# Four mixed layers on one core: value and receptance weights of the second recurrent layer split ahead of time, in earlier feed-forward stages

## The chip, the cores and the metric

The kernel runs on one core of a Trainium2 chip. The core has five engines with a queue of instructions each: PE (the matrix engine, with its weight loads shown as PEld), DVE (elementwise work on 128 partitions), ACT (activations and copies), POOL, and SP, which here only issues DMAs. The metric is the device time of one execution in microseconds, as the median of three runs. The profile is one further execution, taken by the hardware profiler; its own time stands in the table below.

## The reference

The model is a trunk of four residual layers over a sequence of 256 positions with 1024 channels, all in float32. Layers 0 and 3 mix tokens with a recurrence (RWKV-7), layer 1 with stick-breaking attention, layer 2 with sparse attention; a SwiGLU feed-forward block with 2816 hidden channels follows each layer. What matters here is the recurrent mixer. It shifts the input by one position, mixes it with the unshifted one six ways, and multiplies three of the mixtures by 1024x1024 weights:

```
xm = h[:, :, None, :] + (shifted - h)[:, :, None, :] * mix
rkv = jnp.einsum('bsjd,jde->bsje', xm[:, :, :3], w_rkv)
r, k, v = rkv[:, :, 0], rkv[:, :, 1], rkv[:, :, 2]
...
v = v + (v_first - v) * jax.nn.sigmoid(v0 + (xv @ v1) @ v2)   # second recurrent layer
...
state = state * w_t - sa * (kk_t * a_t) + v_t * k_t           # step by step, per head
```

The kernel computes the step-by-step state in chunks of 64 positions: within a chunk a small triangular system is inverted, then the chunks follow each other.

## The kernel before, in words

**Stages.** The program goes through eight stages: mixer 0, feed-forward 0, mixer 1, and so on to feed-forward 3. Activations lie with channels on the partitions. All matrix weights come from DRAM as pieces of 128 x 1024 float32 (512 KB), in the order in which they are needed.

**Two ways to multiply.** A product with float32 weights can be done directly: `product` loads a piece as it is (tile `raw`) and PE multiplies float32 by float32. Or it is done with split operands: a value is taken apart into a high part, rounded to the format fp32r, and the rest, its low part; three fp32r matmuls (high by high, high by low, low by high) replace one float32 matmul (`mm3`, called by `gemm2`). For this `piece` loads a piece into `raw`, ACT or DVE copies it into `wh` (the high part, a CAST), and DVE subtracts the high part from the piece into `wl`. `raw`, `wh` and `wl` have three buffers each. In both recurrent layers the receptance product (tiles `rp`, weights of key `rr`) and the key product (`kp`) use split operands, and the value product (`vp`, key `rv`) is the direct one.

**The inverse.** After the products that make them, the chunk matrices `sc` are masked, and a chain of 62 small DVE operations (tiles `inv` and `xtmp`) inverts their 32x32 blocks. Two DVE transposes end it (`xd`, then `XT`), and PE takes the blocks further with small matmuls (`cmb`). Then the chain over the chunks runs (`xu`, `qu`, `pS`, `Y`), and the output product (`po`) ends the stage. While DVE works on the inverse, PE has the value product and the value's layout changes (`qct`, `vtok`, `bv`).

**Order.** Every operation is recorded first, with what it depends on. The order in which the recorded operations are emitted, the engine of each operation that two engines can do (CAST by ACT or DVE, for instance), and the buffer of each tile stand in one packed table, ORDER, read by `schedule`. Where the table holds an empty turn, `emit` puts in two short matmuls whose result nobody uses (`warm_o`), to keep PE busy. Each engine works its own list strictly in order, and waits for others by semaphores. All DMAs are on SP's queue: a DMA there that waits for a buffer holds back all DMAs behind it.

**Names.** In the order's rows and the profile, out<-in stands for the tile that is written and those that are read; the program's lines for these operations are all in one helper, L571.

Of the kernel before, what the change touches and what calls it, by code (L numbers as in the profile page):

```python
# [24 lines left out]
P = 128  # L25
# [277 lines left out]
c-rk+OKe={b@uuH|Ni&=m^*Xl{U$j>4u?YyDU#wtq9l^yLlPyKl3%iE*|IGsshhfX(k4NgxLKrW<HRXY6m?q!LHs~cv_KXO(mF*K0lIOJHYkv0*Pz|D-  # L303
6flD`u+Fbp(MvhS6!7yCg(o>*E#1q-
#KUKhe~ff^nlPqCvqbH*OECg!HJy6iJZuZoXCls$cdcDiJZuZoX7{|<V%?oIgt}NkrO$Q|A#U?<d#Kb7{)_U#G3bt0x2Kzvq2`n1*FrF6Jcms!Zc0CamJi>8&_s%nno^
H)PgbH&OMfcMA0<^zw}GSrTzT_-7w4Ltm$Q3&+rbzVQ<dWZQSXht_RV0R5MJ&-
7*Z<ivm3=I$l=Sop5S;dQvxZbG+9xqac&Z1sQ*=Qtds{Yc{HtsoD$^Bs5W|6)RUQGn?I97h+Xg5n?R}1G8nD&x^_(!+pkC40@0`O%7yU2s@LpsnHl469wTKi}ku8^g^K
^3?qu9%x1@V_``0d6*m8-*W1^orl$H^?aihB^t2U-$;oQht5qP`Y}KoHUOr#^dNIH$va{JNZ^#Vi-R^j2a@_Mg!5xvy)gvB;U-
+FbTA%$a=ls*Uo^|!W_Vu!5aVZVSU*s@7#IdoAA;i(qW7g4=u{>(>9sTg|5EFNI|6p(b^}WmdA})8Iy>#pO-QDN!93AcM@_TaQ2ETdb;qN{C@WGYKN9Q2xJ8W%jZF6mH
<$H{=>+AzEG0oVS`yUjGY~riq<-&rxdFX+$)6>(EwOg&uWTDXM)R_=0Yd0G8TD?=NjgODpRZUdO^|~plT+{4Qu~gDDEfaChwzs##kg-  # L310
5FeABsh&2>G`xOB<=oNMpyIgWktBA~RjZEWiL`SU=+*^PeRU~{_8mY3N=MfeM2{`?RkgzNTPfs+U!tnu-
VDca*>?KWFl>i1j90D2X+RG<39M6H&?Ri<8Ng+frybDV^0j+U{QX)-mqpm5AERy}v{fC2u7@B8I4gZuLO%#5qBJh{OIlWWpo_65zzY-FnQY*?AA=%UnL=+F0urMWp>LI
)@7I84`pS^eTg9a?WU8fM2V7RSc)GLwLkWNc+coX(ZY12zL;{XQ$yfuj7?t1M!dbNN_UIVzRlzF~IG4%gNkhEpspElmZy%#0#qGP3%8v6`(i1;sEN8ZFi=7<r>wt$N-
#XUtw%S@{jdmJyr4`_MO+o8~jms4a(Pzwc(VS#zpX3d5`6!NL4%`8;Qq6^58x*5T`yU)ETTv05N2lFfTV&(j72jrDC?h_94Zzx-
# [260 lines left out]
def trunk(ctx: ExitStack, tc: tile.TileContext, xT_in, wts, lora_in, consts_in, id32_in, outT, order, layers=None):  # L575
# [358 lines left out]
    def rwkv(j, layer, after):  # L934
# [910 lines left out]
```

## Time and profile before

| what | value |
|---|---|
| median of three runs | 1280.58 us (1278.81 to 1280.99) |
| the profiled execution's own time | 1280.3 us |
| its span, first to last instruction | 1278.5 us |
| PE busy | 1268.4 us |
| DVE busy | 1146.4 us |
| ACT busy | 699.7 us |
| DMA: bytes moved | 221.89 MB, 174 GB/s on average |

The span is read as a row of stages, each with its own busiest engine. The stages' limits, found from the first and last instructions of each, are about: mixer 0 from 8 to 175 us, feed-forward 0 to 350, mixer 1 to 455, feed-forward 1 to 630, mixer 2 to 758, feed-forward 2 to 932, mixer 3 to 1100, and feed-forward 3 to the end. Busy time of matmuls is modelled at its end: a row's mean duration holds the overlap with its neighbours, so a price for PE's time is read from stretches of equal matmuls in the chain of waits, where start follows start.

### The profile page before, as it was taken

How to read it: one execution, taken by the hardware profiler on the slowest of the kernel's cores; microseconds unless marked ns; L12 is line 12 of the kernel's file. 1: busy time of each engine (PE TensorE's matmuls, PEld its weight loads, DVE VectorE, ACT ScalarE, POOL GpSimd, SP SyncE). 2: the span in 40 equal slices, each digit the busy share in tenths (PEclk: the TensorE clock that was granted, in tenths of full speed). 3: DMA queues.
4: the chain of work that ended last, by engine and by line, in shares of the span. 5: the costliest groups of instructions: out<-in, count | busy, mean ns of one | idle time of the engine just before them, and what ended most of it. 6: DMA issues, size and time to landing. Idle time of an engine off the chain costs nothing.

```text
span 1278.5 us, 25690 instructions
## 1 busy us (share of the span) xinstructions
PE 1268.4 (99%) x10362; PEld 1153.1 (90%) x10362; DVE 1146.4 (90%) x1912; ACT 699.7 (55%) x1254; POOL 14.1 (1%) x18
## 2 busy tenths in 40 slices
PE   8999999999999999999999999999999999999998
PEld 7897899999988999999999899999988888999998
DVE  8998999898889989997899998988799998999885
ACT  5976655443355653443467965454249757654521
POOL 0020000000000000000000000000000000000000
PEclk9999999999999999999999999999999999999999
DMA  6432166665564465565646555655743331666654
GB/s 242 145 125 92 53 212 193 216 191 184 193 199 150 143 204 186 197 211 181 211 151 195 169 170 197 212 196 169 232 160 132 131 96 54 213 203 196 198 185 158
DMA packets 62567, 221.89 MB, mean 174 GB/s; under 512 B 7280, under 2 KB 8688, under 8 KB 62192
## 3 DMA queue, kind: packets, MB, share of 16 engines
q1 hardware_dynamic: 62448, 220.25, 52.6%
q8 instruction: 81, 1.33, 0.4%
q14 instruction: 38, 0.31, 0.1%
HBM read 217.08 MB, written 1.05 MB: 171 GB/s over the span
## 4 chain that ended last, share of the span: by engine, by line
PE 94%; DVE 3%; DMA 2%; issue 1%; ACT 0%; SPq 0%; DVEq 0%; ACTq 0%
PE up L571 18%; PE gate L571 18%; PE dn L571 17%; PE po L571 7%; PE vp L571 4%; PE kp L571 3%; PE rp L571 3%; PE vps L571 3%; PE qk L571 3%; PE z L571 2%; DMA raw<-in_wts_dram 1%; PE sc L571 1%; PE Y L571 1%; PE lora_in L571 1%; DVE wl L571 1%; PE attn_o L571 1%
## 5 line engine op out<-in xcount | busy, mean ns | idle before, releaser
L571 DVE TENSOR_TENSOR wl<-raw,wh 128x1024 fp32r<-128x1024 f32 x285 | 346.9, 1221 | 38.7 <-ACT wh L571 32.4
L571 ACT CAST wh<-raw 128x1024 fp32r<-128x1024 f32 x190 | 199.2, 1050 | 183.7 <-PE dn L571 92.7
L571 PE MATMUL dn<-h,wh 128*128 128x512 f32 (+1 forms) x726 | 233.3, 376 | 0.0
L571 PE MATMUL dn<-h,wl 128*128 128x256 f32 x704 | 191.2, 273 | 0.8 <-DVE wl L571 0.8
L571 PEld LDWEIGHTS dn<-h,wh 128*128 128x128 f32 x726 | 135.7, 189 | 18.0 <-DVE h L571 0.2
L571 PE MATMUL up<-xg,wring 128*128 128x512 f32 x704 | 141.8, 328 | 0.0
L571 PE MATMUL gate<-xg,wring 128*128 128x512 f32 x704 | 140.2, 328 | 0.0
L571 PEld LDWEIGHTS dn<-h,wl 128*128 128x128 f32 x704 | 135.5, 192 | 1.2 <-DVE wl L571 1.1
L571 PE MATMUL up<-xg,wh 128*128 128x512 f32 x352 | 123.6, 382 | 0.0
L571 PE MATMUL gate<-xg,wh 128*128 128x512 f32 x352 | 123.1, 382 | 0.0
L571 PEld LDWEIGHTS up<-xg,wring 128*128 128x128 f32 x704 | 106.1, 191 | 9.3
L571 PEld LDWEIGHTS gate<-xg,wring 128*128 128x128 f32 x704 | 106.1, 191 | 9.1
L571 DVE TENSOR_TENSOR wring<-raw,wring 128x1024 fp32r<-128x1024 f32 x88 | 107.0, 1220 | 7.0 <-ACT wring L571 6.0
L571 PE MATMUL up<-xg,wl 128*128 128x256 f32 x352 | 96.0, 273 | 0.0
L571 PE MATMUL gate<-xg,wl 128*128 128x256 f32 x352 | 96.0, 273 | 0.0
L571 PE MATMUL qk<-xg,wh 128*128 128x256 f32 (+1 forms) x384 | 86.1, 313 | 0.0
L571 DVE CAST wh<-raw 128x1024 fp32r<-128x1024 f32 x95 | 65.3, 688 | 18.0 <-PE dn L571 12.0
L571 ACT COPY gus<-gate 128x256 f32<-128x256 f32 x88 | 32.3, 373 | 88.6 <-PE gate L571 73.8
L571 PEld LDWEIGHTS gate<-xg,wh 128*128 128x128 f32 x352 | 66.6, 189 | 9.2
L571 PEld LDWEIGHTS up<-xg,wh 128*128 128x128 f32 x352 | 66.6, 189 | 9.2
L571 ACT CAST wring<-raw 128x1024 fp32r<-128x1024 f32 x58 | 60.8, 1052 | 20.7 <-DMA raw<-in_wts_dram 15.5
L571 PE MATMUL qk<-xg,wl 128*128 128x256 f32 x256 | 70.3, 275 | 0.0
(321 smaller groups left out, 2674.7 us busy)
## 6 DMA issues: line engine op xcount, KB each, us to landing
raw<-in_wts_dram SPq DMA_DIRECT2D x397, 512.0 KB, 4.1
lora<-in_lora_dram SPq DMA_DIRECT2D x2, 1536.0 KB, 9.9
rhl<-qa SPq DMA_DIRECT2D x32, 64.0 KB, 3.4
lora<-in_lora_dram SPq DMA_DIRECT2D x2, 512.0 KB, 5.4
lg<-in_lora_dram SPq DMA_DIRECT2D x8, 128.0 KB, 3.7
inv<-in_id_dram SPq DMA_DIRECT2D x2, 512.0 KB, 4.2
out_dram<-xt SPq DMA_DIRECT2D x3, 256.0 KB, 2.4
xt<-in_xT_dram SPq DMA_DIRECT2D x1, 660.0 KB, 4.8
```

The costliest lines, as they stand in the source:

```text
L571: getattr(getattr(nc, o.eng), method)(*map(real, args), **{k: real(a) for k, a in kw.items()})
```

## The change

**Parking.** A new function `park` does the split of a weight piece early: it loads the piece, casts and subtracts as `piece` does, but into one tile of 128 x 2 x 1024 (1 MB, in the groups of buffers named s0 and s1), and a DMA writes this tile to a place in DRAM. A table AHEAD says which pieces are parked in which feed-forward stage: four value pieces in feed-forward 0, four value and two receptance pieces in feed-forward 1, six receptance pieces in feed-forward 2. That is all eight `rv` and all eight `rr` pieces of layer 3. When `piece` is asked for a parked key, it issues two DMAs of 512 KB, one into `wh` and one into `wl`; no CAST and no subtraction follows.

**Value product.** In layer 3 (j == 1) the value product becomes a `gemm2` with split operands. Its input `xv` is split into high and low parts in a new tile `xvhl`, four times 128 x 512. The first recurrent layer keeps the direct product.

**Tiles.** The inputs of the gate product, `xg`, get a tile of their own in group s0, in both recurrent layers; `XT` moves from s0 to s1, and the two `yhl` tiles swap s0 and s1. The table ORDER is new as a whole.

```diff
     def piece(key, raw=None, parts=None):
 
+        if key in parked:
+            h, l = T([PIECE], "wh", "wh", F32R), T([PIECE], "wl", "wl", F32R)
+            sp.dma_start(f(h), parked[key][:, 0])
+            sp.dma_start(f(l), parked[key][:, 1])
+            return h, l
...
+    def park(key, group):
+
+        i = len(order)
+        order.append(key)
+        r = T([PIECE], "raw", f"raw{i}")
+        sp.dma_start(r, wts[i])
+        plan.ops[-1].lag = 300.0
+        st = T([2, PIECE], group, "parts", F32R)
+        anye.copy(st[:, 0], r)
+        dve.tensor_tensor(st[:, 1], r, f(st[:, 0]), op=ALU.subtract)
+        parked[key] = plan.tile(dram, [P, 2, PIECE], F32, None, f"park{i}", "dram")
+        sp.dma_start(parked[key], f(st))
...
+        for i, key in enumerate(AHEAD.get(layer, ()) if not last else ()):
+            park(key, f"s{i % 2}")
...
+        xgs = T([NC, S], "s0", "xg")
...
-                if i % 2 == 0:
-                    x = t2("xg")
-                mix(x[:, i % 2], "mg", i)
-                xg.append(x[:, i % 2])
+                mix(xgs[:, i], "mg", i)
+                xg.append(xgs[:, i])
...
-                mix(xv[:, i], "mv", i)
-                xvs.append(xv[:, i])
+                mix(xv[:, i], "mv", i, j == 1)
+                xvs.append(il(xv[:, i]) if j == 1 else xv[:, i])
...
-        XT = T([32, C], "s0", "XT")
+        XT = T([32, C], "s1", "XT")
...
+        if j == 1:
+            xvhl = T([2, NC, S], "xb", "xvhl", F32R)
+            for c in range(0, NC, 2):
+                split(xvhl[:, 0, c:c + 2], xvhl[:, 1, c:c + 2], xv[:, c:c + 2])
         for n in range(4):
-            vp = product(("rv", j, n), xv, "vp")
+            vp = product(("rv", j, n), xv, "vp") if j == 0 else gemm2(("rv", j, n), lambda c: (xvhl[:, 0, c], xvhl[:, 1, c]), "vp")
...
-            yhl = T([2, 4, S], f"s{1 - half}", "yhl", F32R)
+            yhl = T([2, 4, S], f"s{half}", "yhl", F32R)
...
+AHEAD = {0: [("rv", 1, n, h) for n in range(2) for h in range(2)], 1: [("rv", 1, n, h) for n in range(2, 4) for h in range(2)] + [("rr", 1, 0, 0), ("rr", 1, 0, 1)],
+         2: [("rr", 1, n, h) for n in range(1, 4) for h in range(2)]}
```

**How the order moves.** Three places matter below. The first is PE in mixer 3, where the value work ends and the first `cmb` stands, which reads the inverse's `xd`. Before:

```order
L571 MATMUL pg_11771<-sg_11087,lg1_11297 128x256
L571 MATMUL pg_11773<-sg_11087,lg1_11297 128x256
L571 MATMUL cmb1_11788<-xd_11786,SB_11122 32x32 x16
L571 MATMUL bv_11815<-UV_11598,SB_11339 64x64 x16
L571 MATMUL cmb1_11833<-xd_11786,SB_11122 32x32
L571 MATMUL cmb2_11835<-XT_11042,zs_11808 32x32
```

Now:

```order
L572 MATMUL pg_12004<-sg_11112,lg1_11298 128x256
L572 MATMUL bv_12014<-UV_11892,SB_11431 64x64 x16
L572 MATMUL bv_12031<-UV_11892,SB_11431 64x64 x16
L1706 LDWEIGHTS warm_x_65
L1706 MATMUL warm_o_12050<-warm_x_65 128x256
...
L572 MATMUL cmb1_12069<-xd_12067,SB_11243 32x32 x16
L1706 LDWEIGHTS warm_x_65
L1706 MATMUL warm_o_12089<-warm_x_65 128x256
```

Two groups of `bv`, which before stood behind the first `cmb` and behind the second, now stand ahead of it, and ten unused matmuls (eight ahead, two behind) are put in.

The second place is SP in feed-forward 0, where the first parked piece (number 76) is written out:

```order
L572 DMA raw80_3271<-in_wts_dram 128x1024
L572 DMA raw65_3275<-in_wts_dram 128x1024
L572 DMA park76_3277<-parts_2583 128x2048
L572 DMA raw67_3338<-in_wts_dram 128x1024
L572 DMA raw78_3367<-in_wts_dram 128x1024
```

The write stands 13 rows behind the load of the next parked piece (number 77), between loads for the feed-forward's own products; it was not there before.

The third place is SP in mixer 3, where the weights of the value product are loaded. Before, each piece is one load into `raw`:

```order
L571 DMA raw317_11289<-in_wts_dram 128x1024
L571 DMA lg_11291<-in_lora_dram 128x256
L571 DMA lg_11293<-in_lora_dram 128x256
L571 DMA raw316_11295<-in_wts_dram 128x1024
L571 DMA lg1_11297<-in_lora_dram 128x512
```

Now a piece is two loads, straight into `wh` and `wl`:

```order
L572 DMA wh_11595<-park78_4313 128x1024
L572 DMA wl_11621<-park79_3988 128x1024
L572 DMA wh_11623<-park79_3988 128x1024
L572 DMA wh_11625<-park178_5681 128x1024
L572 DMA lg_11627<-in_lora_dram 128x256
```

A load that went into a `raw` buffer, ahead of a CAST and a subtraction, is now a pair whose buffers PE itself sets free.

More of the change, by code (lines that the diff above doesn't have):

```diff
@@ L370 @@
[L370 to L374 removed]
+c-rk+S&SuTb)NHYwQqN+yYEYP-
+~D#??PYqOnV#;Rp6;2kXYKKVZN|XZ#+HoD1Omo@6T)JN$N>@*gp()+668FDNbmqeB2tJ@Bo;p;FOiItr#wV?j1(#7ud3TUV~CYVA#s#Go?EwW)nEUA{&T+bopY*vBJ<B
@@ new lines @@
+EQ{l4Lqak4#V_9SJXD8PH05(8^*}!M8&_#Yh`GiFnf-MHj2e^TsO~e9g!?2(%=en_c@NWc?XkR+zpiLytCY>&pZz}j9+fcM#n1FK9hN<myvNuE`??fnSxM`UtV-oogq~
+rb*%)HUJ~+tV(3ze=SK;i!5n^}Oa(0NkXP>r{$s{3_N@d-oo~A81v$IZiTB9$|sO4TN)icePh(bQDY1#`fyx@FvpZvNVkK1?d*q-
+XTla|9dsc}~MON@>`mr#(CehbAe3q|>}!t1XW0x^t>TD2+&DOtz|XeTQc``m!BRRh;ge#S6<i@*3HV}w+zq)&PT>FG}U@@1`+&reQH=JUI|`E!n=Q9%XQ$ohItUCrWZC
+)Gu3_u|wIb$_4GX7j%L&IzHa!cdT99Ngiuvb5CLR*0CNPgD|wfamr5-
+h$^zB2EnD(Nz>wS*h3S?RH&CQ_&R=02~^*5#ofg3}Y#3XEK1^v%vJwE1rivF{H{Z0${|ASSSg3$i&8yOvZ!|-ZY9wT*RSE$e`2dbi1@2h?VLvY8Z`1!-!-
@@ new lines @@
+m`o`!JXmiig(rE;V8_no?UJMm>6l6aZr!ht~DTe0z!3ly52b%~?I~4StLG)M<WERzMyrSUrNUw|-
+s>+zaK?s*p34^v7L_95*DYe2=^b;O+=AbcE)ucq%ZM%x`$hksFTB?FvgLFWt=f#;l7HVA{%I6f0M4>QBQ=3wtdiwNf3AMG#YGo~%#6?T<^QY&Np``oiWS3}xVKnX3sf6
+dPHJdAutgR7Ps@G2jBK<Zp42;iRDHxA4@#*dD{WxyT-PzeWy^Sm3iaUFkdWM6JGS8akI>3TnwJh{lVKA7R84T%w(q6Cc;B3XBS)d6cUc=DT+``FHGO1~q_}W?~lTK?XO
+|;ty5f=|X93R9QH??}F6Dr!SwOX~>>S|iLX|Z0^3Tsjh)(V9c2QDxD?n98xDhMV{7#YA>=<V;jYARKZ<kYDY^+ATi$uxP2`+m5snVBgmo0l&qY-
+lqC2y+d!zPHE98Wgu-YpW0&#A3_68SZgaO=65p+V+GR%UC_NT2&p#QS-
@@ new lines @@
+Jv7z|t&RkPEn6kba8deDt4F$)Ysq1;rt4l1B_Si?w>X1zIkFna@L(lSI7449_^tO#pK;4?<46r0hgOS4%AVcg-s_@vRfaz(k^ZtF27TvrHt2No9>F)EC6=QcJrDBYxVh
+0-
+M%9vJ$#6vm+Ep=#IQDmXCJzSJ&UK#Dj&8o_Q8h9|rDI8jmUbg?Mm1WM5dFPSywTtFBPhdM=|H?CZ{;(f;Rs@19q<*JU_laG9)P{0uz8#41$DsoQ|Ck+OV%{}_)oc*&TC
+>-5(<Hn7AzH`-RV_k7cE|sp;%JM4!Fj%QSO)1|1_!{K%Bu9`HJjofFhS1Mn9*bx;MdLf)fqhI%l}x$pI2^tSkd0@)_O(?sSI013eYFKs`TU5@n%QadcgQQRII8-21R-
+jBO2ZQ5JnU}zQe-rg%yp@`xrA797fcL_+1VUt4X88eqIeuJfkgvMOlZw0*8WKY1hg)ndiu>b@%Rr?;yQhw#^7=LmeTwwAbc8s+h~~e`VUR>8qNxUQ);wI>EA7h)Yg_LY
@@ new lines @@
+i))tnOq*SR~Cilx~{r>kYEp<8<Iwh=X&+eQpZhmlc^Lmk7CHakE<I>t%fspJi`tEb(R%^bswfVpU546sdD|CabGc?#G_hO|&9O9E5Vopyxnjv<3$l-
+K#wTrZ!%PlVESeDQl`S|VOEcjSY_q%rn#r|_2>5z8kApUgXkw>mSnY-
+O?PpT6K@57vby~Q89vg+3k?yFWC)rHN?^ShTjh7NX(or8hfU#A?y`P68%?k`{gba3<C2g6h<v#^p(p1rY@8n&<O?Ul>BYsv29UU%0}n+v3uN9Q(TlY`oFFIELcVIa7dO
+x2*8H{eSpzsEkC^by-JRc(~&;IuO7PdKHF<0SoTwuH%fLis@MS>fHrgzyw4pcNX8Jd#x|R?1ulAh#X_*)UZuGW`L{Y}(A%x3+eeR~3eBB#~tFCBPjdlWT?9S@DU2?0RL
+P3|M;<TR43#(Me!vZ(ww*>Mhk|Uh<J7OL#6&Tl4Ltu)#zyLBrBiH4ab&cpTR?AFZX+7_&YG?sX-
@@ new lines @@
+WNJ1QoCQKzRK|tDzi&*)`M#2*;n_cYp5!TuRdou@Z8L0-Ad;+<Euc0zX{EJ-E_^x^`hnZ=4Ih~F#E~etXzr-
+;KXXiYOqfQ48xN1wTx4gV;uf|twD8@PqolYSZgFCXc%L2h(z_tKx-
+!_aY@;GW+EI!<{kZ}$Uy485RjI9vXZTZxmqhdu<vFGPu4mE+*TyA+;(@uIz<&&@oMZ?HHWLdK4vW<>~J<6p^Mo?aYxw9i#JCAv~@fVE-VAtRq3)p`ce_*@@fBe<2Vx*P
+Jv%lA+3Ms^2c}3T~&tr7Ij3k9$)x9dI#C8CXqt7Uk^>jy<_CmuwiJzI7le((S&kqRnW-y3KB~kRem%s(gA60%Haf9T`o_j8SCSG{+%{KvtLuAQ-
+6aoAEH{N&yz3`KtNMB$gRUkw2`72j~mLy-TLPZdc)nG1%mDcO{(b1@~pLSMxob#`6jueSbnVvS4QVa?O`1{i?5SxgX>U9%)UNQ$G{inMA;~%5nawMyvH?^Ql)hdAiX*6
@@ new lines @@
+PW^Z}Q3QZ{QBxK*~Ye`r}q>44PpGQekpqSpz!MeLzGFZW?j%jkOQqaW3@WdB35tbG3YJ9j939#SdrK^FVB15r*rTr9elgCGES5dCmqn%7NCl*3_qLD&7RPpC?X5FM!3u
+`XB%3xhJ8GR*?xD~v4}D$*Dx<+zB&EK8J1sUjGh8<e_eupELAp++@7N3BdIAa1ORyfma_K@Z@mmTH<92(oN)WRW7NRSKTsQB^(fdq48NKN@{^q=iC=sVGxZ3T8X}A@f~
+DDJvx<lyp^5{NMINNvGu-
+CsZ!0#1zj9J0A226(Rr~%ejU@8kTPAhtf^!dh9;N;;5dYSXiLf6eUh#y3DlUkZbzYs|+<^L5eb^zCr0I1eW?(iQ-|nI9%WZ2$Kj=x_GG9<ro$~BoIpDcnJR4l--9KVLx
+M<%pjNsHC@0eh2@pyjb#o+;hTc!#ZLoM6&;nomIhlfvA(os{HYJg>IuuGGmE_^pnH0Km3O*xbNy+<MKr{rLsEXymxg!Uelnd(R*MDSjk%dzawYbX>z(wJ7o3=4J5JsHp
@@ new lines @@
+!KmA63MRhVXSPSQUp?vDH0$C#4;_@wB?bmuH27Xah!$os=dCZSbNLp<>3%}i9ve$B;RH|Tz_sJJ<!%#t>I9*t=Vi%Y0c1u#d4)s(hz4nUv5+x`*@;Ic!GTlVe>Iv=4c_
+XjdxHXg+F6_;A!Li?`KbEo_vx8qPUK%_Ka&330xWzV3&~{xbQC6+q$%~)7l5jzB_ySdk@_F<V&B#)4(}r@bl0HL?YjA!2-
+bC!u;xJWhCYLjqAa!8LZKu3(y9@@}wne6ui(}o0K=3&2UUHH*6sT6eGc4%tJbZu+HW4>1-
+DJB|K00P)vsF&A6WHIIinNe@G54Vzb^nL0P#LK%?9%mr8{;Lc3U)DB`W=MB&|y=A-#~UOM6OW$-g8-+$L5`OHHPap;{&pnb1iV+lW*NF);%E?i_xdIhURi);}KQF-
+c=VQv@(UtL`@bbWzfWl~y%1uP&HWp;LUFqm<}&VQ<{s8bUY6Vosh3k$k@C5J7bCYqAXt3;I1%n8}yrt?@9`Wau%Pon89&Lcpp)KV$-
@@ new lines @@
+4TRET{t*L^DzO8aa46xQ4Mtf+1YSI}i~*A(-r6a13&Q%((Is=t6@B@Si-
+5v<`mBKSs&olQQ`X4+>E^kPAixaO}i`$3adNs4Qoa%i|5ff}rQvZKDqO&GAXb1jli~M^?Ew5Lr&es{(@cIKwT-
+d6+<!!)H);yvIc7G6)q5af{P&ERwOd<+7(II0?Z{5O*oH!5=CY5%Qy&j~;~|kYFOFP^O}t@E4D+!5CL^TXGDMFB}5TpmIde(1VnWaTIJCS70PuNZO1>ZU`Qff9EEFsRT
+aBX+#4oFnf3>m;@~(OS}^VPRNtMtz_&T5)Kprla4_idR;m#7!=)u&>hifH0($YuM(lCXl)*BRqixA;Zn^|b@XCzU0RBY5TAI52X+~AUWB~>K|BaL2|ek>(DXv?lmz1>k
+j6L<tP<cj@H{!he)L8?;x~p$;=FQ`V*CIP_ZF@!PgxYz!IM0SDH?Q15Cw?{p&F<uw@k)5Aa-c5HyUF3FlqzbQn_g8z(~chdx8@@vN0~hEe5lO8zSLOqBDMY8f-
@@ new lines @@
+T7iJ&2gOWnt5>j<C_f=&==f<TSXr)XRWZGnL)LmW{YU{z`>(G>(CXJgYICOx2m<pR($i1cM+H_@?GLKGaiHgH(zE&NYrcnT^*Ja8fZlqDp&ppWr420KSxs44>&u^<9mD
+U7ND4UC~ID26NJ@^KMHRj@D}(_m<@h*aPxUPHv7&I)I$v=$HJ;t&&|C#B~ZjqcF96JNj<k@w}pWK0W0h9sjQC<8tCA^4&@G>l=nfpOxFkR0Ivf)o77L;sBHgAm|H0RrP
+9AbiI=hH#W^#G#2v^rWQ1kih~-k2xizYPp>-tb@OA5E-
+9LS_921HB}<SAy!y`BKZ}9F08^JLMkQ$$+~i8226TINM4rwEO}ADct<k1gr?vO*`JM#M8ib`=;2Kk*)?D^oEYbq4wEgP^e~e;1T0M?*K?{$HVIY{a-
+fh5r$}T|Z0Hf&0f@K+XOPe7IEZ=h-
+b5glBuUBJSbgHJ@Xv8L5es%Wu6rmYK<*7M)JjE$Q^xEQf=`+xbb>T3k<<{9e7G=#+=H11l@2iz1n>AxfHe`V5TuTvWDTe+qM$H{!*xPMf*_8Zdz9q@9m1M9ipn6-
@@ L375 @@
+k4M0m0Rsk$pvl8X_;+i<2}}
 """
@@ L663, in piece @@
         return h, l
+    parked = {}
+    def park(key, group):
[9 more added lines that the diff above has]
+        sp.dma_start(parked[key], f(st))
     def raw_piece(key):
```

96 lines of the change are left out of this document (24 added, 72 removed).

## The prediction

> **What bounds the kernel now.** I read the page first: the busy shares, then the chain of work that ended last.
>
> ```profile
> span 1278.5 us, 25690 instructions
> PE 1268.4 (99%) x10362; PEld 1153.1 (90%) x10362; DVE 1146.4 (90%) x1912; ACT 699.7 (55%) x1254; POOL 14.1 (1%) x18
> PE 94%; DVE 3%; DMA 2%; issue 1%; ACT 0%; SPq 0%; DVEq 0%; ACTq 0%
> ```
>
> PE is busy in 1268.4 of 1278.5 us, and 94% of the chain is PE's. Time is won only where PE has less to do, or where one of its few waits goes. The share of DVE, 90%, warns that a second engine is close. Which engine is close where, a table by stage tells (columns: the stretch, its length, then PE, PEld, DVE, ACT and POOL busy, granted clock, DMA share, GB/s):
>
> ```profile
> 455.00:630.00 175.00, 175.00 (x1077) 161.24 (x1077) 154.33 (x219) 75.20 (x125) 0.00 (x0) 1.00 0.60 196
> 758.00:932.00 174.00, 173.21 (x1065) 159.29 (x1064) 151.54 (x217) 77.21 (x123) 0.00 (x0) 1.00 0.62 200
> 932.00:1100.00 168.00, 166.97 (x2151) 148.15 (x2150) 159.31 (x307) 115.31 (x212) 2.69 (x4) 1.00 0.36 119
> 936.00:1046.50 110.50, 110.50 (x1049) 97.67 (x1052) 107.40 (x213) 77.68 (x136) 2.69 (x4) 1.00 0.39 133
> ```
>
> The first two rows are feed-forward 1 and 2: PE is full, DVE has 20.7 and 22.5 us to spare, ACT is under half, DMA is at 0.6. The third is mixer 3, which the change is about, the fourth its first part, up to the end of the inverse: there DVE is busy for 107.4 of 110.5 us while PE is full. Two engines bound that part at once. That they even meet at its end, the timeline of DVE and the chain show (start, length, what):
>
> ```profile
> 1044.52 2.00 DVE L571 STREAM_TRANSPOSE xd<-inv 128x1024 f32<-128x1024 f32 x1
> 1046.39 1.92 DVE L571 STREAM_TRANSPOSE XT<-inv 128x1024 f32<-128x1024 f32 x1
> 1048.88 1.40 DVE L571 COPY XT<-XT 32x1024 f32<-32x1024 f32 x2
> 1044.49 2.57 PE pg L571 x16
> 1047.06 0.62 PE cmb L571 x32
> 1047.68 1.08 PE bv L571 x32
> 1048.76 0.88 PE cmb L571 x51
> 1050.78 0.77 PE xu L571 x16
> ```
>
> DVE has xd ready at 1046.52; PE ends its last other work (pg) at 1047.06 and starts cmb. PE's list and DVE's list end within 0.5 us of each other. So neither engine's saving counts alone: the stage gains what the slower of the two gains.
>
> **PE's saving.** The direct value product of mixer 3 stands in the chain in five pieces; the key product is a stretch of equal fp32r matmuls of the same width, 256 columns:
>
> ```profile
> 1004.39 1.06 PE vp L571 x4
> 1009.22 6.24 PE vp L571 x28
> 1016.11 1.92 PE vp L571 x8
> 1019.17 12.28 PE vp L571 x56
> 1033.30 7.11 PE vp L571 x32
> 943.25 8.04 PE kp L571 x72
> ```
>
> The five pieces sum to 28.6 us for 128 rows, two of the trace for each of the 64 matmuls. In their place stand 3 x 64 = 192 fp32r matmuls. At 8.04/72 = 0.1117 us they take 21.4 us, so PE has 7.2 us less to do. The receptance product keeps its matmuls, as does everything else on PE but ten warm_o of 256 columns, which I price at the same 0.11 us: 1.1 us. The granted clock of 1.00 in all these stretches leaves nothing to correct.
>
> **DVE's saving.** A DVE instruction starts before the one ahead has ended, so I price by the distance of starts:
>
> ```profile
> 976.97 0.69 DVE L571 TENSOR_TENSOR EF<-EF,di 128x512 f32<-128x512 f32 x1
> 977.57 1.22 DVE L571 TENSOR_TENSOR wl<-raw,wh 128x1024 fp32r<-128x1024 f32 x1
> 978.71 2.34 DVE L571 TENSOR_TENSOR_SCAN L<-chmask,EF 128x512 f32<-128x512 f32 x2
> L571 DVE CAST wh<-raw 128x1024 fp32r<-128x1024 f32 x4 | 2.7, 682 | 0.0
> L571 DVE COPY gT<-pg 128x256 f32<-128x256 f32 x3 | 1.3, 424 | 0.5 <-PE pg L571 0.4
> ```
>
> A subtraction of a piece costs 978.71 - 977.57 = 1.14 us, one of 512 columns 0.60. Up to xd, counted from the stage's first use of `pre`, DVE's list has nine subtractions of pieces fewer: the eight receptance pieces, and one that now stands ahead of the stage. That is -10.3 us. It has four subtractions for xvhl more: +2.4. And the new table gives it work that ACT did: two CASTs for the receptance input (0.4 each, above half of the row's 0.68 for twice the columns), two copies of 512 columns (0.6), and two operations of 256 columns (0.36 each, by the copy's 0.42 less an overlap of 0.06): +2.7. Two small operations of the norm moved ahead: -0.7. The sum is -5.9 us. Of the CASTs of the eight receptance pieces ACT loses most; ACT was busy for 77.7 of 110.5 us and is no bound.
>
> **Where they meet.** Up to cmb PE has 7.2 us less, but the two bv groups that moved ahead (1.08 us each, by their row) and eight of the ten warm_o (0.9) more: it arrives 4.1 us earlier, at 1042.9 on the old scale. xd is ready 5.9 us earlier, at 1040.6. So cmb waits for PE's list, not for xd. Behind cmb the cover has gone: the first bv had covered the copy of the first result (0.74 us on ACT between cmb's end and the next cmb), so of its 1.08 us about 0.9 comes back as a wait beside the two warm_o there. With cmb's 0.62, the 1.08 and the next cmb's 0.88, xu starts at 1042.9 + 2.6 = 1045.5 in place of 1050.78: 5.3 us earlier. DVE allows it: xu needs the copies of XT, which ended at 1050.28; 5.9 us earlier is 1044.4. From xu on, both lists hold the same work. If instead DVE's list were the later one, the stage would gain at most the 5.9; if PE's list were kept free of waits, 7.2 - 1.1 = 6.1. I take **-5.3 us** for mixer 3, between -3 (a wait of 2 us more in the chain, whose `cmb` has the only wait of PE there, 1.0 us) and -7.2.
>
> **The moved splits.** Sixteen subtractions (18.2 us) and sixteen CASTs now lie in feed-forward 0 to 2, at most six in one: 6.8 us of DVE against 20.7 us to spare. Hidden, then, by PE's matmuls; without that cover each would cost its 1.14 us, 18.2 in all. The writes wait for nothing of their own: ahead of each stands a later load that already waited for DVE, as at park76, so they hold SP's queue for their issue alone. What they delay is the transfers behind them: 1 MB at the rate that the row 455 to 630 implies for a full queue, 196/0.60 = 327 GB/s, is 3.2 us, once per write, in a stage that consumes a piece of 512 KB only every 2.6 us (175 us for 66) and holds six split pieces ahead. With 6 x 1.5 MB more the DMA share of a stage rises from 0.60 to 0.77. I take 0.4 us for all three, between 0 and 3.
>
> **Mixer 0 and the tiles.** Mixer 0 keeps its direct product but gets a new order too. XT now takes the buffer of xv, which the value matmuls of mixer 0 read, so DVE may write it only after the last of them. The list does so: its PE order has no value matmul behind the first cmb any more, where there were two. DVE's list up to its xd holds one subtraction of a piece and two operations on `prs` more (1.14 + 0.6 + 0.3 = 2.0 us), work that was done behind xd before. I take 0.3 us, between -1 and +2. The tile for xg only removes waits; 0.
>
> **The parked loads.** This is the new wait. In `piece` the cast and the subtraction stood between load and PE; now PE reads what the DMA lands, and the load cannot start before PE has left the buffer. The tables that show what a load takes:
>
> ```profile
> DMA to landing us min/median/max: 3.3/3.7/5.5
> 940.00:942.00 2.00, 2.00 (x11) 1.75 (x10) 1.97 (x7) 0.39 (x1) 0.00 (x0) 1.00 0.97 399
> 972.00:1002.00 30.00, 30.00 (x254) 26.62 (x255) 29.79 (x46) 27.47 (x48) 1.58 (x2) 1.00 0.28 95
> 1004.00:1042.00 38.00, 38.00 (x361) 32.21 (x359) 36.07 (x84) 19.86 (x31) 0.00 (x0) 1.00 0.39 125
> lora<-in_lora_dram SPq DMA_DIRECT2D x2, 1536.0 KB, 9.9
> ```
>
> The first row is for raw between 972 and 1045 us: a load lands 3.7 us after issue, on queues that are free two thirds of the time. With three buffers, a load for a piece starts when PE leaves the piece three before, and two pieces of 24 matmuls lie between: 2 x 24 x 0.1117 = 5.4 us, with the other matmuls in the list 6.0 to 7.0 for ten of the sixteen pieces, 4.6 at the shortest, more for the rest. A pair lands in 3.7 us plus the second half's transfer, 0.52 MB at 399 GB/s = 1.3: 5.0 us. That fits, and I take 0 in the sum, with the other end in the rivals.
>
> **Sum.** -5.3 + 0.4 + 0.3 = -4.6 us on the profiled execution: span 1273.9, its own time 1275.7 in place of 1280.3. The median of the runs stands 0.3 above that execution, so the forecast is 1276.0. Its own range, from the ends above, is 1273 to 1278.5.
>
> **Rivals.** *The queue becomes the bound.* Mixer 3 now loads 16 MB where it loaded 8. At 327 GB/s a pair takes 3.2 us against 2.7 us of PE. Over the whole 70 us from 972 to 1042 that is 51 us, and fits; but inside the long runs of rp and vp, some eight pieces in a row without other work, 0.5 us is lost on each, 4 us in all: about 1280. For it speaks the feed-forward's rate, against it the 399 GB/s. The Trainium skill, in DMA: Bandwidth & Descriptors, section Specifications, gives about 358 GB/s as the HBM limit of one core; by it a pair would take 2.9 us, and as an estimate half of those 4 us would go. The row with 399 GB/s differs from it, and so I leave it a rival. The same time comes out if parking stalls the feed-forward stages by 4 us.
>
> *The pairs land late: slower than before.* A load of 1536 KB took 9.9 us to land. Between 3.7 us for 512 KB and that, 1 MB would be at 6.8, already at the edge of the 6.0 to 7.0; at 7.5 us, ten pieces would miss by 1 us each, PE would stand for 10 us, and the time would be 1286. It decides from 7.2 us: there ten misses of 0.7 take back the gain and 0.2% more. Against it: that load stood in a busy queue, at the start of a stage.
>
> *More than forecast.* Mixer 3 gains the whole 7.2 us of PE, or a new order elsewhere is better by a wait or two: about 1272.
>
> **How the numbers follow.** Forecast 0.52, the queue or the feed-forward stages eat the gain 0.23, late pairs 0.13, more than forecast 0.12. A measurement of this kernel can tell 0.2%, 2.6 us, from no change: faster is below 1278.0, slower above 1283.1. Faster: 0.50 of the forecast, all of the last rival and 0.02 of the queue's, 0.64. The same: 0.02, 0.19 of the queue's and 0.01 of the late pairs', 0.22. Slower: 0.14. The range for 8 in 10 goes from the last rival to a little beyond the queue's, 1271.5 to 1282.5.
>
> **What would show it.** Right: in mixer 3 the vp rows become 192 of about 112 ns from start to start, xd's end and xu come 5 to 6 us earlier within the stage, PE shows no waits for DMA at rp and vp, and feed-forward 0 to 2 keep 175 us each. Wrong: waits of PE for wh or wl of park (late pairs), feed-forward stages longer by 1 us or more with waits on raw, or cmb waiting for DVE xd by more than 1 us, which would say that DVE's list was mis-summed.

## The result and the profile after

The changed kernel takes 1295.5 us (median of six runs, 1290.9 to 1300.9) where the kernel before, beside it, takes 1279.2 (1278.1 to 1281.0): a ratio of 1.0125, with a 95% interval of 1.011 to 1.014. It is slower by 16.3 us; the forecast was 4.6 us faster.

The page of the changed kernel, its head, the line of its chain of waits by engine, and its DMA issues (out<-in, how many, KB each, median us from issue to landing):

```profile
span 1296.2 us, 25937 instructions
PE 1274.8 (98%) x10434; PEld 1154.0 (89%) x10434; DVE 1160.6 (90%) x1928; ACT 709.4 (55%) x1259; POOL 6.5 (1%) x21
PE 71%; DVE 14%; DMA 10%; ACT 3%; issue 2%; SPq 0%; DVEq 0%; ACTq 0%
raw<-in_wts_dram SPq DMA_DIRECT2D x397, 512.0 KB, 4.2
park<-parts SPq DMA_DIRECT2D x16, 1024.0 KB, 7.8
wl<-park SPq DMA_DIRECT2D x16, 512.0 KB, 5.4
wh<-park SPq DMA_DIRECT2D x16, 512.0 KB, 5.7
```

PE's share of the chain fell from 94% to 71%, and DMA's rose from 2% to 10%. The kernel is no longer bound by PE alone. PE's busy share, 98% against 99% before, hardly shows it, since the ends of matmuls are modelled in it; the share that matters is the one in the chain. The two halves of a parked pair land in 5.4 and 5.7 us at the median. The median of all `raw` loads, 4.2 us against 4.1 before, shows nothing of the trouble: it is the loads right behind a write that are late.

Where the time went, from the first matmul of each stage to the first of the next (us, profiled executions; the last column goes to the last matmul; the kernels of the later rows are told below):

| kernel | to mixer 0 | mixer 0 | feed-fwd 0 | mixer 1 | feed-fwd 1 | mixer 2 | feed-fwd 2 | mixer 3 | feed-fwd 3 |
|---|---|---|---|---|---|---|---|---|---|
| before | 11.0 | 163.4 | 173.3 | 107.7 | 174.5 | 130.2 | 174.6 | 167.0 | 173.6 |
| after | 9.2 | 164.7 | 176.3 | 108.9 | 175.0 | 132.0 | 181.1 | 172.2 | 173.5 |
| nostore | 10.8 | 165.0 | 174.1 | 108.8 | 173.2 | 129.8 | 175.1 | 170.8 | 173.5 |
| nopark | 9.4 | 164.6 | 174.3 | 109.3 | 174.1 | 130.7 | 174.8 | 168.7 | 173.8 |
| half | 9.3 | 164.8 | 175.9 | 108.8 | 177.5 | 132.7 | 179.4 | 169.0 | 173.7 |
| nopark_half | 9.6 | 164.7 | 174.1 | 108.9 | 173.2 | 129.7 | 174.3 | 167.6 | 173.5 |
| store_h | 9.4 | 164.6 | 174.5 | 108.9 | 174.3 | 132.8 | 179.3 | 172.0 | 173.6 |
| before_write | 9.3 | 164.5 | 178.5 | 108.4 | 179.6 | 130.5 | 182.9 | 166.7 | 173.6 |

Feed-forward 0 to 2 lost 10.0 us together, mixer 1 1.2, mixer 2 1.8, and mixer 3 lost 5.2 us where 5.3 were to be won. Two of the sixteen writes do not stay in their feed-forward stage: they are issued at 362.7 us, in mixer 1, and at 644.3 us, in mixer 2; mixer 1's loss also stands in the rows without writes. Each row is one execution: that of the changed kernel took 2.4 us more than its median of six, that of nostore was the fastest of its four. The first two columns together are 174.4 before and 173.9 after: mixer 0 is unchanged.

How a feed-forward stage now looks, in the chain of waits of the changed kernel in feed-forward 2 (start, length, what; idle steps, and DVE's copies `gus` of under 0.5 us, are left out):

```profile
812.12 1.24 DVE wring L572
813.37 7.02 DMA raw<-in_wts_dram
820.42 1.06 ACT wring L572
821.51 0.22 DVE wring L572
822.76 4.94 DMA raw<-in_wts_dram
827.79 0.70 DVE wh L572
828.59 1.24 DVE wl L572
829.84 5.74 DMA raw<-in_wts_dram
835.61 1.06 ACT wring L572
836.70 1.09 DVE wring L572
837.95 4.19 DMA raw<-in_wts_dram
```

Before, from 805 to 850 us, the same part of the stage is one run of matmuls; the chain's shares there:

```profile
by line: PE up L571 51.0%; PE gate L571 45.4%; PE dn L571 4.1%
```

The changed kernel's chain is a ring: DVE's subtraction sets a `raw` buffer free, the load into it lands 4 to 7 us later, then cast and subtraction follow, and the next load starts. PE does not appear in this stretch at all. With three `raw` buffers, a load that takes 4.2 us and about 2.3 us of cast and subtraction the ring turns in 6.5 us and feeds three pieces, where PE needs 2.6 us for each, 7.8 us in all. By this estimate it has 1.3 us of room, and a load that lands later than that uses it up. The landing times of `raw` in feed-forward 1, before and after:

```profile
DMA to landing us min/median/max: 3.4/3.9/6.0
DMA to landing us min/median/max: 3.4/4.3/8.1
```

### The profile page after: what moved, and what is told of

Same layout as the page of the kernel before. It is cut to its first block, busy times and chain, and to the rows that moved or that the text cites. A ratio compares the mean times of both kernels' runs of the same rounds, so it can differ in the third digit from the quotient of the medians.

```text
span 1296.2 us, 25937 instructions
## 1 busy us (share of the span) xinstructions
PE 1274.8 (98%) x10434; PEld 1154.0 (89%) x10434; DVE 1160.6 (90%) x1928; ACT 709.4 (55%) x1259; POOL 6.5 (1%) x21
## 4 chain that ended last, share of the span: by engine, by line
PE 71%; DVE 14%; DMA 10%; ACT 3%; issue 2%; SPq 0%; DVEq 0%; ACTq 0%
PE up L572 13%; PE dn L572 13%; PE gate L572 13%; DMA raw<-in_wts_dram 8%; PE po L572 7%; PE qk L572 6%; PE kp L572 3%; PE vps L572 3%; DVE wl L572 3%; PE z L572 2%; PE rp L572 2%; DMA wh<-park 2%; DVE gus L572 1%; PE Y L572 1%; DVE inv L572 1%
## 5 line engine op out<-in xcount | busy, mean ns | idle before, releaser
L572 DVE TENSOR_TENSOR wl<-raw,wh 128x1024 fp32r<-128x1024 f32 x277 | 338.0, 1224 | 42.5 <-ACT wh L572 34.9
L572 ACT CAST wh<-raw 128x1024 fp32r<-128x1024 f32 x185 | 193.3, 1048 | 187.8 <-DMA raw<-in_wts_dram 79.8
L572 PEld LDWEIGHTS up<-xg,wring 128*128 128x128 f32 x704 | 106.1, 190 | 10.8 <-DVE wring L572 1.7
L572 ACT CAST wring<-raw 128x1024 fp32r<-128x1024 f32 x62 | 65.1, 1050 | 41.3 <-DMA raw<-in_wts_dram 41.0
L572 DVE CAST wh<-raw 128x1024 fp32r<-128x1024 f32 x92 | 63.4, 689 | 19.8 <-PE dn L572 10.2
```

The lines of the kernel that those rows point to most:

```text
L572: getattr(getattr(nc, o.eng), method)(*map(real, args), **{k: real(a) for k, a in kw.items()})
```

## The experiments

Two theories stood at the start. The first: each write of 1 MB makes the loads behind it late, and the feed-forward stages have no room for that. The second: the parked pairs land too late in mixer 3. The rivals: the split work itself, or the new order, or DVE's list. The code cuts below tell each edit in short: an operation that is left out or replaced keeps its place in the order, and the order is otherwise that of the changed kernel. "+x" below is the median less that of the kernel before in the same set (1280.9, 1281.5 and 1282.0 us in the three sets); the changed kernel is at +16.3.

**No writes (nostore).**

```diff
-        sp.dma_start(parked[key], f(st))
+        if len(parked) == 1: sp.dma_start(parked[key], f(st))   # mixer 3 reads this pair for all
```

> Of the sixteen writes of the changed kernel only the first is left; the loads, casts and subtractions ahead of them stay, and all sixteen pairs of mixer 3 are read from that one place in DRAM (so receptance and value are computed with one piece's weights; the loads are as many and as large as before). Theory: each write of 1 MB stands in the one queue ahead of a load of 512 KB that is needed just in time, and makes it 2 to 3 us late; then feed-forward 0 to 2 fall from 176.3 / 175.0 / 181.1 us to at most 174.5 / 174.5 / 175.5, mixer 3 stays at 171 to 173, and the time falls from 1295.5 to about 1286. Rival: the split work itself (sixteen casts on ACT, sixteen subtractions on DVE) or the new order makes the stalls; then the three stages keep most of their 9 us and the time stays above 1292.

Measured: 1287.8 us (1286.0 to 1290.4), +6.9; ratio 1.0060 (1.0041 to 1.0078). Feed-forward 0 to 2 take 522.4 us together in the profiled execution, to the tenth what they took before, though all loads, casts and subtractions of parking are still in them. So the writes cost 9.4 of the 16.3 us by the medians, and in this execution the split work costs these stages nothing. Mixer 2 is back at 129.8 us too.

**Half pairs (half).**

```diff
             sp.dma_start(f(h), parked[key][:, 0])
-            sp.dma_start(f(l), parked[key][:, 1])               # wl: the wh buffer is read again
```

> In mixer 3 the second half of each of the sixteen pairs is not loaded; the matmuls of that half read the first half again (so the low parts of the weights are wrong). The writes stay as in the changed kernel. Theory of late pairs: with 8 MB instead of 16 a piece lands in about 3.7 us, the waits of PE for the two park loads at the receptance and value matmuls go, and mixer 3 falls from 172.2 to about 165 us, the whole to about 1288. Rival: mixer 3 is held by DVE's list (xd, XT and the copies ahead of xu), not by the pairs; then it stays within 2 us of 172. On feed-forward 0 to 2 both expect nothing: 176, 175 and 181 us, within 1.5.

Measured: 1294.8 us, +13.9. Mixer 3 falls by 3.2 us, to 169.0, and not by 7: up to `cmb` it is 4.3 us shorter, and the stretch from `xu` to `po` is 1.1 us longer, by the clock that is told below. Late pairs are real, but they are less than half of the 10.5 us that mixer 3 misses.

**Neither (nopark_half), and no parking but whole pairs (nopark).**

```diff
     def park(key, group):
+        if len(parked) >= 1: no load, no cast, no subtraction, no write
```

> Both left out: of the sixteen parked pieces only the first is loaded, split and written, and in mixer 3 each pair loads one half only, from that one place. What remains is the new order, the new tiles and the value product by three fp32r matmuls in place of the direct one, with the splits of xvhl. If the writes, the split work and the pairs are all of the loss, this takes what the prediction had said of PE's and DVE's savings: about 1273 us, mixer 3 at 161 to 163. If the new order itself carries waits, it stays above 1279, with feed-forward 0 to 2 above 174.5 us each.

> Of the sixteen parked pieces only the first is loaded, split and written, and all sixteen pairs of mixer 3 are read whole from that one place (so receptance and value are computed with one piece's weights). Against the kernel without writes (feed-forward 0 to 2 at 174.1 / 173.2 / 175.1) this shows what the loads, casts and subtractions of parking cost there: by the theory nothing, 173.5 to 175 each. Against the kernel with halved pairs and no parking (mixer 3 167.6) it shows what late pairs cost: by the theory mixer 3 is at 170 to 171.5 us, 3 to 4 us more. The whole: 1285. Rival for mixer 3: the splits that it no longer has to share DVE with set it; then it is at 168.

Measured: nopark_half 1282.4 us (1280.0 to 1284.6), +1.5, ratio 1.0008 (0.9996 to 1.0019); nopark 1285.4 us (1282.6 to 1286.2), +3.9, ratio 1.0030 (1.0018 to 1.0042). This is the most telling pair. With no write, no split work ahead and half the loads, what is left of the change is only its gain, and it gains nothing: mixer 3 is at 167.6 us. The whole pairs cost 2.4 us more in the median; in the stretch up to `cmb` 114.8 against 111.3 us. Mixer 3 as a whole is at 168.7 us in nopark, below the 170 to 171.5 expected, because its stretch from `xu` to `po` is 2.4 us shorter than in nopark_half (the clock again). In nopark feed-forward 0 to 2 take 523.2 us, in nostore 522.4: by the profiles the split work is free there. By the medians it is less sure: nostore, which has the split work of fifteen pieces more, is at +6.9 and nopark at +3.9, with intervals that just meet (from +5.3, and up to +5.4).

Why mixer 3 gains nothing even then stands in nopark_half's chain of waits and in PE's own waits up to there:

```profile
934.75 0.86 PE lora_in L582 x4
1007.95 2.88 PE vp L582 x24
1012.11 2.88 PE vp L582 x24
1015.63 5.55 PE vp L582 x48
1021.83 5.55 PE vp L582 x48
1028.03 5.55 PE vp L582 x48
1045.91 0.72 PE cmb L582 x32
PE bv L582 <- ACT UV L582: 1.1, 1, 1.1
PE warm_o L1724 <- ACT QC L582: 0.7, 1, 0.7
```

From the stage's first matmul `cmb` comes after 1045.91 - 934.75 = 111.2 us; before, from the row `934.91 0.87 PE lora_in L571 x4` to 1047.06, after 112.15. It is 1.0 us earlier, not 4.1. The value matmuls take 22.4 us (2 x 2.88 + 3 x 5.55), 1.0 more than priced, and PE stands 1.1 us for ACT's copies `UV` and 0.7 for `QC`; 4.1 - 1.0 - 1.1 - 0.7 = 1.3, which leaves 0.3 us unexplained. The wait for `UV` has its reason in ACT's timeline, of before and of nopark_half:

```profile
1032.69 1.18 ACT L571 COPY UV<-vtok 64x512 f32<-64x512 f32 x2 [11.57 <-PE vtok L571]
1034.40 0.58 ACT L571 COPY UV<-vtok 64x512 f32<-64x512 f32 x1
1035.73 0.57 ACT L571 COPY UV<-vtok 64x512 f32<-64x512 f32 x1
```

```profile
1034.70 2.26 ACT L582 COPY UV<-vtok 64x512 f32<-64x512 f32 x4 [3.43 <-PE vtok L582]
```

Before, the four copies began 7.7 us ahead of the end of the last value matmuls (1040.41), under their cover. Now they begin behind them, at 1034.70, where the value matmuls end at 1033.58. What ended ACT's wait by the trace is PE's `vtok`, whose result it copies: the new order has the first `vtok` behind the last value matmul, where before it stood ahead of it (1031.45). The code gives a reason for this place: the new tile `xvhl`, which every value matmul reads, and `UV` are both of the group xb, one buffer, so no part of `UV` can be written until the last value matmul is done. With an earlier `vtok` the copies could then begin 1.1 us earlier at most. No run tests this by giving `UV` another buffer.

DVE's list is late too. Its transpose `xd` in nopark_half, and its busy time up to there (columns as in the prediction's windows):

```profile
1042.86 1.97 DVE L582 STREAM_TRANSPOSE xd<-inv 128x1024 f32<-128x1024 f32 x1
934.75:1044.83 110.08, 108.30 (x1185) 98.56 (x1185) 104.94 (x217) 66.94 (x123) 2.23 (x4) 1.00 0.40 137
934.91:1046.52 111.61, 111.61 (x1055) 98.65 (x1057) 108.48 (x215) 77.70 (x136) 2.69 (x4) 1.00 0.40 134
```

The third row is the same stretch before. DVE's work fell by 3.5 us, not 5.9, and 2.0 of that came back as idle time (5.1 us against 3.1): xd is 1.5 us earlier. It is ready 110.1 us into the stage, so even without PE's two waits `cmb` could not come more than 2.1 us earlier than before.

**Writes in quarters (chunk), later (late), on another queue (actq).**

```diff
-        sp.dma_start(parked[key], f(st))
+        chunk: four of 128 x 512 columns, one behind each of four loads, from two loads later on
+        late:  whole, on SP's queue, three loads later
+        actq:  whole, on ACT's queue, two loads later
```

> Nothing left out. Each write of 1 MB is cut into four of 256 KB that are issued behind four successive loads, the first of them two loads later than the whole write was. If what hurts is that one load waits behind a whole megabyte, each load is now late by at most 0.8 us, the stalls go, and feed-forward 0 to 2 lose some 7 of their 9 us: about 1288. If what hurts is the total of the traffic or the split work, the three stages keep their times and the whole stays at 1293 to 1297.

> Nothing left out. Each write of 1 MB stays whole and stands three loads later in the queue. Theory of the total: a write costs the loads behind it some 3 us of lateness together, whichever loads these are, and all loads of a feed-forward stage are equally just in time; then feed-forward 0 to 2 stay at 176 / 175 / 181 us within 3 us and the whole at 1293 to 1299. Rival: the writes stand ahead of the wrong loads, or hold the queue themselves while they wait for DVE's subtraction; then the three stages lose at least half of their 9 us and the whole falls to 1290 or less.

> Nothing left out. Each write is issued by ACT, on ACT's own queue, two loads later than before. If what costs is that the loads stand behind the write in one queue, they now pass it, a load lands at most 1 us later than without a write, and the time falls to 1286 to 1290, near the 1287.8 of the kernel without writes. If what costs is the share of the 16 DMA engines that the write takes (2.5 us for 1 MB at their full rate), the same lateness is spread over two or three loads and the time stays at 1293 to 1299; ACT's own wait for DVE may add to it.

Measured: chunk 1309.2 us (+28.3), late 1305.2 (+23.7), actq 1304.2 (+22.7). All three are worse than the changed kernel, where each was expected to be equal or better. Two of them mix changes: chunk and actq also move the writes two loads later. How late loads are, by their place behind a write (mean us from issue to landing in feed-forward 2, read from the traces' issue and landing times; before: 4.14 for all):

| kernel | the write | 1st load behind | 2nd | 3rd | loads not among the 5 behind a write |
|---|---|---|---|---|---|
| after | 8.1 | 6.8 | 5.6 | 4.4 | 4.3 |
| late | 7.2 | 6.5 | 5.9 | 4.4 | 4.3 |
| actq | 6.0 | 6.1 | 5.0 | 4.4 | 4.4 |
| chunk | 5.7 | 5.4 (each quarter) | | | 4.4 |
| store_h | 6.4 | 5.7 | 4.7 | 4.2 | 4.4 |
| readback | 7.5 | 6.6 | 5.5 | 4.2 | 4.4 |
| before_write | 7.0 | 6.6 | 5.8 | 3.8 | 4.4 |

In feed-forward 2 of the changed kernel a write of 1 MB makes the load behind it 2.5 us late and the second one 1.3, against its other loads. On ACT's own queue it is still 1.7 and 0.6: the loads no longer stand behind the write in a queue, but they share the same DMA engines with it. The Trainium skill says so in DMA: Bandwidth & Descriptors, section Queues, rings and completion order: SP's and ACT's queues are rings on the same 16 engines, served in turn; the row of actq agrees, with 6.1 us behind a write of the other queue. Quarters make four loads late by 1.0 us each in place of two by 2.5 and 1.3. That is no less in sum, and it spares no load.

Why the place matters: how long a load lies landed before its cast starts. Over the 195 loads of feed-forward 0 to 2 before, the quartiles are 0.31, 1.01 and 1.75 us, and 43 casts start within 0.2 us of the landing. In nostore, with the parked pieces among the 212 loads, they are 0.08, 0.42 and 1.03; in the changed kernel 108 of 211 casts start within 0.2 us. A lateness of 2.5 and 1.3 us fits under no such slack. Late changes the place alone and costs 7.4 us more than the changed kernel, so the order has its writes at better places than three loads later. The 6.4 us more of actq and the 12.0 of chunk cannot be parted into place and queue, or place and size; which loads have the slack at each place was not traced one by one.

**Read in place of write (readback), half the write (store_h), writes alone (before_write).**

```diff
-        sp.dma_start(parked[key], f(st))
+        readback: sp.dma_start(f(st), first_pair)               # 1 MB, the other direction
+        store_h:  sp.dma_start(parked[key][:, 0], f(st[:, 0]))  # 512 KB
+    before_write, in the kernel before, behind every 10th or 7th load:
+        nc.sync.dma_start(copy, xv[:, :NC * S])                 # 1 MB, sixteen times
```

> Fifteen of the sixteen writes are turned round: at the same place in the queue, as large as they were, a read of 1 MB from the first parked pair into the buffer that the write read (nothing uses it then); all pairs of mixer 3 are read from that first place (so receptance and value are computed with one piece's weights). Theory: the cost is the time of the 16 DMA engines, 8 KB in 0.309 us per engine, 2.5 us for 1 MB, whatever the direction; then the loads right behind land at 6 us or more as they do behind the writes, feed-forward 0 to 2 stay at 176 / 175 / 181 us within 3, and the time is 1293 to 1297. Rival: it is the direction (a write must be confirmed in HBM, or HBM turns round slowly); then it is near the 1287.8 of the kernel without writes, at most 1290.

> Fifteen of the sixteen writes carry the first half of the pair only, 512 KB (the second halves of all pairs are read from the first parked pair, so those weights' low parts are wrong). If lateness goes with the bytes, half of the 7.7 us between the changed kernel and the one without writes is saved: about 1291.5. If each write costs the same whatever its size, as the four times as many writes of a quarter of the size suggested (1309.2), it stays at 1294 to 1297.

> The kernel before, with sixteen writes of 1 MB added (the residual input, 8 KB of each partition, into sixteen places in DRAM that nobody reads): four in feed-forward 0, six each in 1 and 2, behind every tenth or seventh load. Nothing is left out, and nothing else of the change is in. Theory: a median load of these stages lands 0.8 to 1.2 us before its cast begins, and a write makes the next load 2 us late and the one behind it 1 us, so most writes cost PE 0.5 to 1 us: 1289 to 1297. Rival: the kernel before has the room, and the stalls need the changed kernel's order or its extra loads and splits; then the time is within 2.6 us of 1280.9.

Measured: readback 1297.9 us (+16.0), store_h 1291.7 (+9.7), before_write 1299.9 (+17.9; ratio 1.0145, 1.0124 to 1.0166). The direction does not matter: a read of 1 MB at the same place costs what the write does. The bytes do: half of them cost 2.8 us above nostore's +6.9, where all cost 9.4. Which half costs more stays open, since in feed-forward 0 to 2 of the profiles half the bytes cost 5.6 of 10.0 us. And the kernel before has no room either: sixteen writes, with nothing else of the change, cost 17.9 us, more than the 8 to 16 expected, 1.1 us each, all of it in feed-forward 0 to 2 (541.0 us against 522.4). The chain of before_write shows the ring of the changed kernel (eight steps between 804.3 and 811.3 us are left out):

```profile
795.25 6.69 DMA raw<-in_wts_dram
802.02 1.05 ACT wring L572
803.10 1.23 DVE wring L572
811.31 1.23 DVE wring L572
812.55 5.97 DMA raw<-in_wts_dram
```

**The clock (warm).** In the profile after, TensorE's granted clock is no longer 1.00 throughout. Windows of the changed kernel around xu, and one of before at the same place:

```profile
1061.60:1068.40 6.80, 4.72 (x196) 3.75 (x197) 2.93 (x5) 4.65 (x13) 0.00 (x0) 1.00 0.01 2
1068.40:1075.20 6.80, 6.26 (x145) 5.62 (x140) 4.81 (x8) 3.62 (x9) 0.00 (x0) 0.50 0.21 69
1053.80:1060.60 6.80, 5.90 (x155) 4.92 (x156) 4.63 (x10) 3.00 (x10) 0.00 (x0) 1.00 0.26 85
```

PE was busy in 4.72 of 6.80 us, and for the next 6.8 us the clock was halved. PE's waits between 1050 and 1070 us, which lie ahead of it or in it:

```profile
PE xu L572 <- ACT XT L572: 1.3, 1, 1.3
PE bv L572 <- ACT UV L572: 1.1, 1, 1.1
PE warm_o L1706 <- ACT QC L572: 0.7, 1, 0.7
PE cmb L572 <- ACT zs L572: 0.2, 1, 0.2
```

```diff
+        for name, more in (("bv", 5), ("cmb", 3), ("xu", 5)):   # pairs of warm_o ahead of the first of each
+            ops[at:at] = [None] * more
```

> Nothing left out; 26 warm_o matmuls of 256 columns (2.9 us) are added in mixer 3, ahead of the first bv, the first cmb and the first xu, where PE stood waiting for ACT for some 3.6 us in all. Theory: those waits make the clock gate halve TensorE's clock for 6.8 us behind them (the clock's record of the changed kernel has 0.5 from 1068.4 to 1075.2 us, the one of before nothing), and that is the 1.9 us by which the stretch from xu to po grew; then the record shows no 0.5 in mixer 3, and xu to po falls from 30.4 to about 28.5 us, while cmb comes at most 1 us later. Rival: the stretch is longer by its own waits on DVE's pr, Sn and u; then it stays at 30 whatever the clock does. On the whole time both expect less than its measurement can tell.

Measured: 1298.2 us (+16.7), in the whole no change. The granted clock of its four runs is 0.999 or 1.000, so the halved clock is not what made the changed kernel slower than the one before. It stays at 1.00 in mixer 3:

```profile
1058.00:1072.00 14.00, 12.23 (x389) 10.31 (x384) 8.65 (x14) 8.82 (x22) 0.00 (x0) 1.00 0.07 10
```

The stretch from xu to po falls from 30.4 to 28.2 us, as expected; but vp to cmb grows from 40.5 to 42.0, so 2.9 us of filler won 0.7. All profiles together say the same: the stretch is 28.0, 28.1, 28.2, 28.2 and 28.5 us where the clock was never halved in mixer 3 (nopark, actq, warm, before_write, before), 29.2, 29.2 and 29.3 where it was for 3.4 us (chunk, late, readback), 30.4, 30.5 and 30.4 for 6.8 us (after, nostore, nopark_half), 31.5 and 31.6 for 10.2 us (half, store_h). A third of the halved time is lost. The Trainium skill, in TensorE: Matmul & The Clock Gate, Part 1, tells of a gate that watches PE in windows of about 3.4 us and halves the clock after an idle one; the multiples of 3.4 us agree. Its rule for kernels, no idle gap above some 3.4 us, was kept here and was not enough: the longest single gap ahead was 1.3 us, and the clock was halved all the same.

## Why the prediction was wrong

**The moved splits: the step that failed most.** It priced the writes at 0.4 us, between 0 and 3; they cost 9.4. That a write waits for nothing of its own stands (each is issued within 0.06 us of the instruction ahead of it on SP), and so, nearly, does its transfer time (3.2 us forecast; in feed-forward 2 the loads behind are late by 3.8 together). What failed is the cover, a stage that "holds six split pieces ahead". Six split pieces do not help when the load that refills the ring is itself just in time: the ring sets the pace, and a load's slack, from its landing to its cast, was 1.0 us at the median. This could have been read from the trace of before, by the time from each landing to its cast. The first rival named this mechanism, at 4 us, "if parking stalls the feed-forward stages"; its size was less than half.

That the split work, 18.2 us of DVE, hides under PE's matmuls was right by the profiles of nostore and nopark (522.4 and 523.2 us, 522.4 before); the 3.0 us between their medians leave a part of it open.

**Mixer 3, forecast -5.3 us.** Without writes and with half pairs it is +0.6. PE's own saving was nearly right, 28.6 to 22.4 us for 21.4 forecast. The failed step is "cmb waits for PE's list", with the list taken free of waits: 1.8 us of waits for UV and QC stand in it, the first because `vtok` now stands behind the last value matmul, for which the buffer that `xvhl` shares with UV is the likely reason. I had seen the ten warm_o and priced them as work of 1.1 us; eight of them stand where PE waits for QC, and an empty turn in the table may be a wait that the order had foreseen (no run tests this). DVE's -5.9 was -3.5 in busy time and -1.5 at xd, which alone would have held the gain at `cmb` to 2.1 us in place of 4.1. And behind xu, where "both lists hold the same work", the stretch is 1.9 us longer by the halved clock; the prediction had taken the clock of 1.00 from rows of before.

**The parked loads, forecast 0.** They cost 2.4 us in the median and, up to `cmb`, 3.5 in the profile. The three longest transfers in mixer 3's chain of the changed kernel, PE's waits for pairs, and the state of the DMA engines there:

```profile
1005.25 7.38 DMA wh<-park
1020.79 6.24 DMA wh<-park
1033.97 7.43 DMA wh<-park
PE rp L572 <- DMA wl<-park: 1.0, 1, 1.0
PE vp L572 <- DMA wl<-park: 0.9, 1, 0.9
PE vp L572 <- DMA wh<-park: 0.8, 2, 0.6
PE rp L572 <- DMA wh<-park: 0.4, 1, 0.4
1005.00:1015.00 10.00, 8.64 (x102) 8.14 (x99) 10.00 (x18) 5.15 (x8) 0.00 (x0) 1.00 0.81 316
1015.00:1030.00 15.00, 14.67 (x174) 13.61 (x172) 12.87 (x25) 10.79 (x16) 1.89 (x2) 1.00 0.84 297
```

I had priced a pair at 5.0 us from loads that had queues free two thirds of the time; pairs in a row fill the engines to 0.81 and 0.84, and the `wh` loads between 1000 and 1050 us then land in 4.0 to 7.9 us, 6.5 at the median. PE's waits for them sum to 3 us. The price had to come from a busy stretch. The queue's rival had the right cause and nearly the right size, "4 us".

**Mixer 0 and the tiles, forecast +0.3:** right within 1 us, the stretch up to feed-forward 0 is 0.5 us shorter. Of the tiles, XT and xg cost nothing that mixer 0 shows; the one that may have cost time, `xvhl` in xb, was not looked at.

In sum: forecast -4.6. Measured +16.3, of it writes 9.4, pairs 2.4, the order with all its gain 1.5 (in place of -5.0), and 3.0 between nostore and nopark. What the two kernels differ in is the split work, but whether it cost these 3.0 stays open: in their profiles, which are 1.2 us apart, the feed-forward stages are equal within 1 us, and the clear difference is mixer 3 (2.1 us), where nostore had the halved clock and nopark had not.

No version beat the kernel before: the best, with everything costly taken out, is no faster than it.

## What to carry to other kernels

Before a transfer is added to a queue that feeds an engine just in time, read the slack: from each landing to the first use of what landed. An average DMA share of 0.6 is no slack when every second load is used within 1 us. A saving on a full engine is worth only what the waits in its list and the list of the next engine leave of it: check for each new tile which later tile shares its buffer, and ask of filler in a written order whether it covers a wait.

## What the runs showed of the hardware

A transfer of 1 MB delays the loads behind it whether it is a read or a write, and also from another queue: in feed-forward 2 of the five kernels with 1 MB the first load behind is 1.7 to 2.5 us late and the second 0.6 to 1.5, with the least on ACT's queue; a quarter of it delays one load by 1.0, not 0.6. And in mixer 3 TensorE's clock was halved for 3.4 to 10.2 us though no single gap of PE shortly ahead was above 1.3 us; it did so in some kernels with the same waits and not in others (nopark has the same three waits of 1.3, 1.1 and 0.7 us, and kept its clock).
